# Eight of sixteen gates by Strassen's scheme in a third pass of the values' stage, and the first products of an output between the last head's jobs

## The chip, the cores and the metric

The kernel runs on one core of a Trainium2 chip. The metric is the device time of one launch in microseconds (us). The engines are named as in the profile: PE multiplies matrices, DVE (VectorE) and ACT (ScalarE) work on elements and empty PE's accumulators (PSUM), POOL and SP here mostly issue transfers.

## What is computed

One layer of a decoder on 1024 tokens of width 1024. The part that matters here, cut from the reference:

```python
h = rms_norm(x, pre_mix_g[l])
proj = h @ w_in[l]
qa, ka, va, qb, kb, vb, gates = jnp.split(proj, split_at, axis=-1)
oa = diff_attention(rope(qa), rope(ka), va, lam)        # A: 4 heads, two softmaxes each
ya = (rms_norm(oa, diff_head_g[l]) * (1.0 - lam_init)).reshape(b, s, A_WIDTH) @ w_a_out[l]
outs, lses = [], []                                     # B: 3 dilations x 4 heads
for g, (window, dil) in enumerate(B_PAIRS):
    o_g, lse_g = dilated_group(rope(qb)[:, :, g], rope(kb)[:, :, g], vb[:, :, g], window, dil)
...
yb = (softmax over g of lses, times outs).reshape(b, s, B_WIDTH) @ w_b_out[l]
g_a, g_b = jnp.split(jax.nn.sigmoid(gates), 2, axis=-1)
x = x + rms_norm((g_a * ya + g_b * yb) @ w_mix_out[l], post_mix_g[l])
... # then a conv-gated MLP, not touched by the change
```

The gates are 2048 columns of `proj`: `g_a` (the first output's) is 1024 of them, `g_b` the others.

## The kernel before

Every large product is made of three float32r matmuls (`mm3`, lines 155 to 157): each operand is held as a rounded high part and a low part, and high x high, low x high and high x low are summed in one PSUM bank. ACT makes the high part, DVE the low one (`split`, line 148; `L149` and `L146` in the profile). A full matmul is 128x128 weights against 512 columns.

The span falls into stages that follow each other.

The values' stage (0 to about 165 us of the span) makes the attention's values by Strassen's scheme: seven products `p1` to `p7` in place of eight, each of four steps k. A table `steps_v` sets the order. It runs two passes, i = 0 and i = 1, of 1024 columns each. `fetch_v` loads the weights' blocks, `ready_v` combines and splits them, `step_v` does the matmuls, and at k = 3 `take_v` empties the four banks into `quarter` tiles, which `put_v` scales and stores on POOL's queue to `v_d`.

Attention A (about 205 to 538 us) runs four heads, each of eight jobs `attend_a(h, i)`, i being a block of 128 queries. A job computes scores `s` on PE into one of two PSUM buffers (`L759`, `L760`, chunks of up to 512 keys), DVE masks them and takes the maximum while it copies them out (`L762`), ACT takes the exponential (`L771`), DVE combines the two softmaxes (`L778`), PE transposes the result (`L691`, `pt<-ident,s`), ACT and DVE split it, and PE multiplies it by the values (`L704`, `L707`). The norm of half a head (`head_norm`) has a sum over partitions on PE (`L833`, `o<-ones,sq`), a chain of small DVE operations (`L166` to `L179`), a spread (`L836`) and a product (`L842`).

Between the jobs stand pieces of independent products, the fills: the next head's projections (`proj_a`, letter p; each has 192 matmuls `acc<-xh` and `acc<-xl`), the first projection of attention B (P), and gates (g, 48 matmuls each, evacuated by DVE at `L250` and stored to `gt_d`). `A_FILLS` lists the fills of each head; `START_GATES` gates run ahead of the first head. `interleave` spreads the fills over the jobs by weight, and a scheduler orders each engine's instructions from priorities and its own estimate of times.

Attention B (about 538 to 870 us) has twelve steps of four jobs `attend_b`, with the next step's projection (`proj_b`) as fill, and `B_GATES` gates in the last one. Its results go through DRAM and are merged over the dilations (`merge`: load statistics `mr`, weights `me`, store them to `e_d`, load them back broadcast as `mw`, multiply and add in two halves; `L1054` to `L1089`), then split to `obh` and `obl`. The first output's products (`branch(a["w_a_out"], ...)`, `ya`, `L1190`) run after the last step's jobs; steps of the merge are called between them by numbers (`later(n, fn)`). Then come the second output, the mix and the MLP.

Three lines that set the order around the change:

```python
START_GATES, A_FILLS, B_GATES = 1, ("gpgg", "gpvgg", "wgpgg", "xgPVgg"), 3
steps_v += [(p, i, k) for i in range(2) for p in ("p1", "p5", "p6", "p7", "p4", "p3") if i or p != "p1" for k in range(4)]
for i, fn in zip((3, 5, 7, 11, 16), merge(BH - 1, ob)):
```

Of the kernel before, what the change touches and what calls it, by code (L numbers as in the profile page):

```python
# [54 lines left out]
XT_BUFS, NORM_AT, ANGLES_AT, SINES_AT, TABLES_AT, STORE_AT = 6, 14, 25, 33, 34, {35: 0, 37: 3, 39: 2, 41: 1}  # L55

# [6 lines left out]
def plan():  # L63

    order = []
    for h in range(AH):
        order += [QA + h * P, KA + h * P]
    for h in range(BH):
        for g in range(BG):
            order += [QB + g * 512 + h * P, KB + g * 512 + h * P]  # L70
    order += [GT + i * P for i in range(2 * KC)]
    return order
# [15 lines left out]
def trunk(ctx: ExitStack, tc: tile.TileContext, a, out):  # L88
# [355 lines left out]

    with ExitStack() as st_y:
# [3 lines left out]
        steps_v = [(p, 0, k) for k in range(4) for p in ("p2", "p1")] + [("p2", 1, k) for k in range(4)]  # L449
        steps_v += [(p, i, k) for i in range(2) for p in ("p1", "p5", "p6", "p7", "p4", "p3") if i or p != "p1" for k in range(4)]  # L450
        wz = [t[:, k % 2] for t in [wv.tile([P, 2, 512], F32, tag=f"wz{i}", name="wz") for i in range(2)] for k in range(2)]
# [37 lines left out]
        def take_v(p, i, m, ps):  # L489
# [3 lines left out]
            def copy(to, r):  # L493
                if i:
                    nc.scalar.activation(to, ps, AF.Copy, scale=r)
                else:
                    nc.scalar.activation(to, ps, AF.Copy)

            def add(to, r):
                if i:  # L500
                    plus(to, ps, r, to, ALU.add)
                else:
                    tt(to, ps, to, ALU.add)
# [5 lines left out]
            if p == "p6":  # L509
                copy(quarter[1, i][m], r1)  # L510
            if p == "p7":
                copy(quarter[3, i][m], r1)
            if p == "p4":
# [4 lines left out]
        def put_v(q, i, scale):  # L518

            c, j = q // 2, q % 2  # L520
            for m in range(4):
# [6 lines left out]
        banks, fifth = {}, {}  # L528

        def step_v(n):  # L530
# [16 lines left out]
            if p == "p7":  # L547
                for m in range(4):
                    r, y = rstd[:, 4 + m : 5 + m], quarter[3, i][m]
                    if i:  # L550
                        plus(y, banks[False][m], r, y, ALU.add)
                    else:
                        tt(y, banks[False][m], y, ALU.add)

# [50 lines left out]
        yw = open_pool(st_y, "yw")  # L605
        made, fetched, again = 12, 14, []
        quarter.update({(q, 0): new_y(f"b{q}", yw) for q in range(1, 4)})
        for n in range(8, len(steps_v)):
# [23 lines left out]
            if n == TABLES_AT:  # L632
                turn_norms()
            if (p, i, k) == ("p6", 1, 0):
                quarter[1, 1] = new_y("a0")
                quarter[3, 1] = new_y("b3", yw)
                quarter[2, 1] = new_y("b2", yw)
            step_v(n)
            if k == 3 and i and p in ("p1", "p7", "p4"):
                put_v({"p1": 0, "p7": 3, "p4": 2}[p], 1, p == "p1")  # L640
            if (p, i) == ("p5", 1):

                again.append(load_raw(a["xT"][k][:, 512:], next(tags)))
            if (p, i) == ("p6", 1):
                with behind_marks():
                    split_x(k, halves()[1], again[k])
        put_v(1, 1, False)
    st_v.close()
# [69 lines left out]
    def proj_a(h, res):  # L718
# [128 lines left out]

    free_gates = list(range(2 * KC))

# [34 lines left out]
    def once(fn):  # L884

        fn()
        yield 0
# [234 lines left out]
    for n, (pair, g, h) in enumerate(steps[:-1]):  # L1122
# [3 lines left out]
        if h % 2:  # L1126
            fetch_b(*nxt[:2])
        fill = proj_b(nxt[1], nxt[2], ops_b[nxt], functools.partial(split_b, *nxt[:2]) if h % 2 else None)
        interleave(jobs(todo), 4, (itertools.chain(fill, once(load_ots)) if nxt == steps[-1] else fill, 8))
        if pair == 1 and g < 2 and h == 2:  # L1130
# [5 lines left out]
    oa = [[slot(n) for _ in range(AH)] for n in ("oah", "oal")]  # L1136
    load_o(oa, None, 0, 1, ots[0])
    load_o(oa, None, 1, 1, ots[1])
    later(1, lambda: load_o(oa, oa_d, 2, 2, ots[0]))
    later(1, lambda: load_o(oa, oa_d, 3, 2, ots[1]))  # L1140
    ob = []
# [5 lines left out]
    xs.close()  # L1147


    st_o = ExitStack()  # L1150
    st2 = ExitStack()
    ym = open_pool(st2, "ym")
    ya = [ym.tile([P, S], F32, tag=f"y{d}", name=f"ya{d}") for d in range(KC)]
    mid_b = open_pool(st_o, "mid_b")
    ob += [[mid_b.tile([P, S], F32R, tag=f"{n}{h}", name=n) for h in range(BH)] for n in ("obh", "obl")]

    def branch(w_out, o, first, gate_tile, get_psum, scale=None):

        gts = []
        for d2 in range(KC // 2):  # L1160
            wh, wl = load_unit(w_out[d2], scale=scale)
            for e in range(2):
                d = 2 * d2 + e
                while len(gts) < min(d + 3, KC):
                    gts.append(gate_tile())
                    side(gts[-1], gt_d[first + len(gts) - 1])
                with behind_marks():
                    nc.scalar.activation(gts[d], gts[d], AF.Sigmoid)
            for half, sl in enumerate(halves()):
                for e in range(2):  # L1170
                    ps = get_psum()
                    for k in range(4):
                        w = slice(k * 256 + e * P, k * 256 + (e + 1) * P)
                        mm3(ps, wh[:, w], wl[:, w], o[0][k][:, sl], o[1][k][:, sl], k == 0, k == 3)
                    yield 2 * d2 + e, half, sl, ps, gts[2 * d2 + e]


    for h in range(2):
        load_o(ob, ob_d, h, 3 * h + 4)
    for i, fn in zip((3, 5, 7, 11, 16), merge(BH - 1, ob)):  # L1180
        later(i, fn, 0)

# [5 lines left out]

    for d, half, sl, ps, gt in branch(a["w_a_out"], oa, 0, gate_slot, psum, ghead):
        marks["DVE"] = nc.vector.tensor_tensor(ya[d][:, sl], ps, gt[:, sl], op=ALU.mult).ins  # L1190
        clock[0] += 1
        while due and due[0][0] <= clock[0]:
            do_due()
# [18 lines left out]
    with st2:  # L1212
        wm = open_pool(st2, "wm", side="right")
        us = [None] * 8
        with st_o:
# [4 lines left out]

            for d, half, sl, ps, gt in branch(a["w_b_out"], ob, KC, gate_tile, any_psum):
                nc.vector.tensor_tensor(gt[:, sl], ps, gt[:, sl], op=ALU.mult)
                nc.gpsimd.tensor_tensor(gt[:, sl], gt[:, sl], ya[d][:, sl], op=ALU.add)
                split(mh[:, d, sl], ml[:, d, sl], gt[:, sl])
                for i in MIX_UNITS.get(d, ()) if half else ():

                    to = (wm, ("mh", "ml"), 4) if i < 4 else (ym, (f"y{2 * i - 8}", f"y{2 * i - 7}"), 1)
                    us[i] = load_unit(a["w_mix_out"][i], *to)
# [467 lines left out]
def layout(inp):  # L1696
# [8 lines left out]
    w = f["w_in"][0]  # L1705
    arr["w_v"] = np.concatenate([w[:, VA:QB], w[:, VB:GT]], 1).reshape(KC, P, 2048)
    us = []
# [33 lines left out]
```

## Time and profile before

| what | us |
| --- | --- |
| median of 3 runs | 1707.98 (1705.85 to 1708.24) |
| the profiled execution, its own time | 1705.22 |
| its span, first to last instruction | 1703.2 |
| PE busy | 1683.8 (99%) |
| DVE busy | 1346.0 (79%) |
| ACT busy | 888.4 (52%) |
| POOL busy | 108.7 (6%) |

The span is shorter than the execution's time by 2.0 us. Matmuls overlap: a row of matmuls gives the time from the start of one to its end, and the rate is read from how many start in a window. Idle time of an engine costs something only where PE, busy for 99% of the span, then waits too.

### The profile page before, as it was taken

To read this page: it belongs to the slowest core of one execution; us is meant where nothing else is said; L and a number is where in the kernel's file an instruction comes from. 1 tells how busy PE (TensorE), PEld (TensorE's weight loads), DVE (VectorE), ACT (ScalarE), POOL (GpSimd) and SP (SyncE) were. 2 spreads that over 40 slices of the span, in tenths; PEclk is the share of its full clock that TensorE was granted. 3 is DMA by queue.
4 is the path that set the end of the run, shared out by engine and by line. 5 is a ranking of instruction groups with operands and counts; after the bars stand their busy time and mean duration, and the time that the engine had idled before them with its cause. 6 is when DMAs were issued, how large, how long until landed. Compare 5 with 4: busy or idle time off the path is not lost.

```text
span 1703.2 us, 23027 instructions
## 1 busy us (share of the span) xinstructions
PE 1683.8 (99%) x8076; PEld 1408.2 (83%) x8076; DVE 1346.0 (79%) x2557; ACT 888.4 (52%) x1631; POOL 108.7 (6%) x174
## 2 busy tenths in 40 slices
PE   9999999999999999999999999999999999999997
PEld 7887888888888888888878788888888888888886
DVE  8895686877777776678756865899999999799977
ACT  7634574655544776667553443454444434355453
POOL 0031000000000000000123400300000000000000
PEclk9999999999999999999999999999999999999999
DMA  8677321214112213243675631122222222296624
GB/s 270 228 231 253 98 63 62 83 59 119 50 63 81 69 57 108 81 123 107 214 259 193 198 112 75 38 99 91 95 80 81 81 93 93 79 345 214 202 76 160
DMA packets 104451, 216.41 MB, mean 127 GB/s; under 512 B 12992, under 2 KB 22144, under 8 KB 104336
## 3 DMA queue, kind: packets, MB, share of 16 engines
q1 hardware_dynamic: 89296, 171.28, 30.5%
q0 software_dynamic: 10288, 35.28, 6.2%
q10 hardware_dynamic: 4752, 8.39, 1.3%
q8 instruction: 63, 1.03, 0.2%
q14 instruction: 52, 0.43, 0.1%
HBM read 167.05 MB, written 47.86 MB: 126 GB/s over the span
## 4 chain that ended last, share of the span: by engine, by line
PE 89%; DMA 5%; DVE 3%; issue 2%; ACT 1%; POOL 1%; SPq 0%; DVEq 0%; ACTq 0%; POOLq 0%
PE acc L155 20%; PE acc L157 19%; PE acc L156 19%; PE acc L1577 3%; PE acc L1576 3%; PE acc L1575 3%; PE o L704 2%; PE pt L691 2%; PE acc L1256 2%; PE acc L1254 2%; PE acc L1255 2%; PE o L707 1%; PE s L156 1%; PE s L157 1%; PE s L155 1%
## 5 line engine op out<-in xcount | busy, mean ns | idle before, releaser
L155 PE MATMUL acc<-xh,whi 128*128 128x512 f32 x768 | 304.2, 396 | 0.0
L157 PE MATMUL acc<-xl,whi 128*128 128x512 f32 x768 | 303.8, 396 | 0.0
L156 PE MATMUL acc<-xh,wlo 128*128 128x512 f32 x768 | 303.1, 395 | 0.0
L149 ACT ACTIVATE whi<-raw 128x512 fp32r<-128x512 f32 (+1 forms) x252 | 155.9, 626 | 185.9 <-PE acc L157 107.6
L146 DVE TENSOR_TENSOR wlo<-raw,whi 128x512 fp32r<-128x512 f32 (+1 forms) x252 | 180.7, 723 | 44.2 <-ACT whi L149 40.5
L157 PEld LDWEIGHTS acc<-xl,whi 128*128 128x128 f32 x768 | 144.4, 188 | 27.7
L156 PEld LDWEIGHTS acc<-xh,wlo 128*128 128x128 f32 x768 | 144.5, 188 | 27.6
L155 PEld LDWEIGHTS acc<-xh,whi 128*128 128x128 f32 x768 | 144.4, 188 | 27.4 <-DVE t L679 0.2
L155 PE MATMUL acc<-mh,whi 128*128 128x512 f32 x400 | 155.8, 390 | 0.3 <-ACT mh L149 0.3
L156 PE MATMUL acc<-mh,wlo 128*128 128x512 f32 x400 | 155.6, 389 | 0.0
L157 PE MATMUL acc<-ml,whi 128*128 128x512 f32 x400 | 155.3, 389 | 0.0
L678 ACT ACTIVATE t<-acc 64x512 f32<-64x512 f32 (+1 forms) x160 | 94.7, 592 | 58.5 <-PE acc L157 56.6
L1452 DVE TENSOR_TENSOR u<-acc,u 128x512 f32<-128x512 f32 x133 | 90.4, 683 | 22.7 <-PE acc L157 22.6
L149 ACT ACTIVATE whi<-s 128x512 fp32r<-128x512 f32 x76 | 46.9, 627 | 102.1 <-PE acc L157 88.0
L679 DVE TENSOR_TENSOR t<-acc,cos 128x512 f32<-128x512 f32 x64 | 44.2, 690 | 58.8 <-ACT t L678 58.0
L155 PEld LDWEIGHTS acc<-mh,whi 128*128 128x128 f32 x400 | 75.1, 188 | 15.9 <-ACT mh L149 0.5
L157 PEld LDWEIGHTS acc<-ml,whi 128*128 128x128 f32 x400 | 75.1, 188 | 15.7
L156 PEld LDWEIGHTS acc<-mh,wlo 128*128 128x128 f32 x400 | 75.1, 188 | 15.6
L1576 PE MATMUL acc<-whi,wlo 128*128 128x512 f32 x220 | 77.6, 390 | 0.0
L1575 PE MATMUL acc<-whi 128*128 128x512 f32 x220 | 76.3, 389 | 0.0
L1577 PE MATMUL acc<-wlo,whi 128*128 128x512 f32 x220 | 73.2, 390 | 0.0
L762 DVE CUSTOM_DVE_ANT_0 s<-s,mask_a 128x512 f32<-128x512 f32 (+3 forms) x96 | 51.9, 553 | 23.3 <-PE s L760 14.6
(385 smaller groups left out, 3942.6 us busy)
## 6 DMA issues: line engine op xcount, KB each, us to landing
raw<-in_w_in SPq DMA_DIRECT2D x96, 256.0 KB, 2.9
raw<-in_w_up SPq DMA_DIRECT2D x88, 256.0 KB, 2.8
raw<-in_w_v SPq DMA_DIRECT2D x71, 256.0 KB, 4.7
raw<-c_d SPq DMA_DIRECT2D x48, 256.0 KB, 3.6
c_d<-c SPq DMA_DIRECT2D x22, 512.0 KB, 2.8
raw<-in_w_down SPq DMA_DIRECT2D x37, 256.0 KB, 4.5
v_d<-yv POOLq DMA_DIRECT2D x32, 256.0 KB, 5.5
gt_d<-gate ACTq DMA_DIRECT2D x32, 256.0 KB, 2.1
```

The source lines that it names most:

```text
L146: eng.tensor_tensor(lo, src, hi.bitcast(F32), op=ALU.subtract)
L149: copy = nc.scalar.activation(hi, src, AF.Copy)
L155: nc.tensor.matmul(o, sh, mh, start=first, stop=False, skip_group_check=on)
L156: nc.tensor.matmul(o, sl, mh, start=False, stop=False, skip_group_check=on)
L157: nc.tensor.matmul(o, sh, ml, start=False, stop=last, skip_group_check=on)
L678: nc.scalar.activation(t1[dst], ps[src], AF.Copy)
L679: nc.vector.tensor_tensor(t2, ps, cos[:, sl], op=ALU.mult)
L762: nc.vector.tensor_tensor_reduce(out=s_sb[:, c0:c1], in0=ps, in1=mask, scale=1.0, scalar=-3.0e38, op0=ALU.add, op1=ALU.max, accum_out=mx[: ...
L1452: nc.vector.tensor_tensor(to, made(p), x, op=ALU.add)
L1575: nc.tensor.matmul(banks[m], gh[:, tk], wh, start=f == 0, stop=False)
L1576: nc.tensor.matmul(banks[m], gl[:, tk], wh, start=False, stop=False)
L1577: nc.tensor.matmul(banks[m], gh[:, tk], wl, start=False, stop=f == NH - 1)
```

## The change

The values' stage gets a third pass, i = 2, which makes the eight gates of the first output by the same seven products. There the operands of `mm3` change places (the gates are wanted transposed), `put_g` multiplies the quarters by the row norm and stores them to `gt_d` on POOL's queue. The passes i = 1 and i = 2 run two products at a time in turns, so that the last step of one stands well ahead of the first step that reuses its banks. `w_v` is widened by these 1024 columns, and the same columns leave the layout of `w_in`. Loads of 256 KB from `w_v` go from 71 to 107, those from `w_in` from 96 to 80. Of the eight gates that are left, none runs ahead of the first head, seven are fills of attention A (there were 12 with the one ahead of it), and one runs in attention B's last step (there were 3).

In attention A the duplicated low halves of k (16 subtractions on DVE, 64x512) become copies on ACT. In attention B's last step four outputs (48 matmuls) of the first output's `branch` stand between the jobs, behind the gate; the rest of that generator runs after the jobs. Its sigmoids thus stand among the last exponentials, and ACT's table loads go from 9 to 11. The numbers of the last head's merge become 3, 5, 6, 9 and 12. In the second output the four banks of the first two columns are begun with k < 3 before the last head's product k = 3 (`late=True`).

```diff
-START_GATES, A_FILLS, B_GATES = 1, ("gpgg", "gpvgg", "wgpgg", "xgPVgg"), 3
+A_FILLS, B_GATES, B_OUTS = ("gpg", "gpvg", "wgpg", "xgPV"), 1, 4
...
+        for i in (1, 2):
+            steps_v += [("p1", 1, k) for k in range(4)] if i == 1 else turns(2, (0, 0, 1, 0, 1, 0, 1, 1), "p2", "p1")
+            steps_v += turns(i, (0, 0, 1, 0, 1, 0, 1, 1), "p5", "p6") + turns(i, (0, 0, 1, 1, 1, 1, 0, 0), "p3", "p7")
+            steps_v += [("p4", i, k) for k in range(4)]
...
+        def put_g(q):
+
+            c, j = q // 2, q % 2
+            for m in range(4):
+                y, sl = quarter[q, 2][m], halves()[j]
+                tt(y, y, rstd_row[:, sl], ALU.mult)
+                nc.gpsimd.dma_start(gt_d[c * 4 + m][:, sl], y)
...
-                mm3(use[m], x[0][:, k, tk], x[1][:, k, tk], wh, wl, k == 0 and p in ("p1", "p2", "p5"), k == 3, p in ("p6", "p7", "p4", "p3"))
+                ops = (x[0][:, k, tk], x[1][:, k, tk], wh, wl) if i < 2 else (wh[:, tk], wl[:, tk], x[0][:, k], x[1][:, k])
+                mm3(use[m], *ops, k == 0 and p in ("p1", "p2", "p5"), k == 3, p in ("p6", "p7", "p4", "p3"))
...
-            for part, kk, ll in ((u, k0, l0), (v, k1, l1)):
-                for to in (u, v):
-                    nc.vector.tensor_tensor(ll[to, sl], t[part], kk[part, sl].bitcast(F32), op=ALU.subtract)
+            for part, other, kk, ll in ((u, v, k0, l0), (v, u, k1, l1)):
+                nc.vector.tensor_tensor(ll[part, sl], t[part], kk[part, sl].bitcast(F32), op=ALU.subtract)
+                nc.scalar.activation(ll[other, sl], ll[part, sl].bitcast(F32), AF.Copy)
...
-        run(gates(START_GATES)[0])
...
+            if late and d2 == 0:
+                for half, e in todo:
+                    begun[half, e] = get_psum()
+                    products(d2, half, e, range(3), begun[half, e])
...
-    interleave(jobs(todo), 4, gates(B_GATES))
+    outputs, size = outputs_a(), 4 * B_GATES + B_OUTS
+    interleave(jobs(todo), 4, (part(outputs, size), size))
...
-    for i, fn in zip((3, 5, 7, 11, 16), merge(BH - 1, ob)):
+    for i, fn in zip((3, 5, 6, 9, 12), merge(BH - 1, ob)):
...
-            for d, half, sl, ps, gt in branch(a["w_b_out"], ob, KC, gate_tile, any_psum):
+            for d, half, sl, ps, gt in branch(a["w_b_out"], ob, KC, gate_tile, any_psum, late=True):
```

Where the order of instructions changes is seen at two places. The first is the border of heads 1 and 2 in attention A. On PE before, from the sum of a head's norm (`o<-ones,sq`) on, the matmuls `acc<-xh` and `acc<-xl` of the fills stand between the scores' chunks `s<-k,q`:

```order
L833 MATMUL o<-ones,sq 128x1 x4
L759 MATMUL s<-k_2977,q_2975 128x128
L760 MATMUL s<-l_2979,q_2975 128x128
L156 MATMUL acc<-xh,wlo 128x512
L157 MATMUL acc<-xl,whi 128x512
L155 MATMUL acc<-xh,whi 128x512
L156 MATMUL acc<-xh,wlo 128x512
L759 MATMUL s<-k_2978,q_2976 128x512
L760 MATMUL s<-l_2980,q_2976 128x512
L157 MATMUL acc<-xl,whi 128x512
L155 MATMUL acc<-xh,whi 128x512
L156 MATMUL acc<-xh,wlo 128x512
```

On PE after, the chunks of head 2's first jobs follow one another, with nothing between but one norm's transposes (`spread`), transposes of the last jobs of head 1 and their products with the values:

```order
L780 MATMUL s<-k_3463,q_3461 128x384
L781 MATMUL s<-l_3465,q_3461 128x384
L780 MATMUL s<-k_3462,q_3460 128x512
L781 MATMUL s<-l_3464,q_3460 128x512
L780 MATMUL s<-k_3462,q_3460 128x512
L781 MATMUL s<-l_3464,q_3460 128x512
L862 MATMUL pt<-ident,spread 128x128 x4
L712 MATMUL pt<-ident,s 128x128 x3
L780 MATMUL s<-k_3463,q_3461 128x512
L781 MATMUL s<-l_3465,q_3461 128x512
L725 MATMUL o<-pt,vh 128x256
L780 MATMUL s<-k_3463,q_3461 128x512
```

On DVE after, at the same place, the masks (`s,mx<-s,mask_a`) stand among the splits of the next values (`vl`), of transposes (`pt`) and of head 3's q, and the combination of 896 keys:

```order
L783 ISA s,mx<-s,mask_a 128x512
L783 ISA mx 128x1
L783 ISA s,mx<-s,mask_a 128x512
L783 ISA mx 128x1
L147 TENSOR_TENSOR vl<-vperm,vh 128x1024
L747 TENSOR_TENSOR q_4220<-t_4291,q_4220 64x512
L799 SCALAR_TENSOR_TENSOR s<-s,ratio 128x896
L748 TENSOR_TENSOR q_4221<-t_4291,q_4221 64x512
L747 TENSOR_TENSOR q_4220<-t_4393,q_4220 64x512
L787 TENSOR_TENSOR mx<-mx 128x2
L748 TENSOR_TENSOR q_4221<-t_4393,q_4221 64x512
L783 ISA s,mx<-s,mask_a 128x512
```

A chunk's matmuls can start only when the mask of the chunk two before it has emptied the buffer; what moved out from between them is independent work of PE.

The second place is the end of head 3, where attention B begins (`s<-kh,qh` are B's scores, which have no fill ahead of them either). On PE before, fills go on past the seventh of the eight sums of A's norms:

```order
L833 MATMUL o<-ones,sq 128x1 x4
L155 MATMUL s<-kh,qh 128x256
L156 MATMUL s<-kh,ql 128x256
L157 MATMUL s<-kl,qh 128x256
L157 MATMUL acc<-xl,whi 128x512
L155 MATMUL acc<-xh,whi 128x512
L156 MATMUL acc<-xh,wlo 128x512
```

On PE after, the next fill behind the same sum stands only after products with the values, the norm's transposes and those of the next block:

```order
L725 MATMUL o<-pt,vh 128x256 x2
L728 MATMUL o<-pt,vl 128x256
L725 MATMUL o<-pt,vh 128x256 x2
L725 MATMUL o<-pt,vh 128x128 x2
L728 MATMUL o<-pt,vl 128x128
L728 MATMUL o<-pt,vl 128x256
L862 MATMUL pt<-ident,spread 128x128 x4
L712 MATMUL pt<-ident,s 128x128 x3
L156 MATMUL acc<-xh,whi 128x512
```

The gates that were this head's last fills are gone from it, and its projection stands further ahead.

More of the change, by code (lines that the diff above doesn't have):

```diff
@@ L70, in plan @@
             order += [QB + g * 512 + h * P, KB + g * 512 + h * P]
-    order += [GT + i * P for i in range(2 * KC)]
+    order += [GT + i * P for i in range(KC, 2 * KC)]
     return order
@@ L510, in take_v @@
                 copy(quarter[1, i][m], r1)
+            if p == "p5" and i:
+                copy(quarter[3, i][m], r1)
             if p == "p7":
-                copy(quarter[3, i][m], r1)
+                (add if i else copy)(quarter[3, i][m], r1)
             if p == "p4":
@@ L546, in step_v @@
                     take_v(p, i, m, use[m])
-            if p == "p7":
+            if p == "p7" and i == 0:
                 for m in range(4):
[L549 to L553, printed above, removed]
+                    tt(quarter[3, 0][m], banks[False][m], quarter[3, 0][m], ALU.add)
         with ExitStack() as st0:
@@ L1127, in trunk @@
             fetch_b(*nxt[:2])
-        fill = proj_b(nxt[1], nxt[2], ops_b[nxt], functools.partial(split_b, *nxt[:2]) if h % 2 else None)
-        interleave(jobs(todo), 4, (itertools.chain(fill, once(load_ots)) if nxt == steps[-1] else fill, 8))
+        between = load_ots if nxt == steps[-1] else functools.partial(split_b, *nxt[:2]) if h % 2 else None
+        interleave(jobs(todo), 4, (proj_b(nxt[1], nxt[2], ops_b[nxt], between), 8))
         if pair == 1 and g < 2 and h == 2:
@@ new lines, in trunk, with gate_slot, outputs_a @@
+    first_gls = iter(("cos", "sin"))
+    def gate_slot():
+        tag = next(first_gls, None)
+        return tabs.tile([P, S], F32, tag=tag, name="gl") if tag else slot("gl", dt=F32)
+    def outputs_a():
+        yield from gates(B_GATES)[0]
+        xs.close()
+        ym.append(open_pool(st2, "ym"))
+        ya.extend(ym[0].tile([P, S], F32, tag=f"y{d}", name=f"ya{d}") for d in range(KC))
+        mid_b = open_pool(st_o, "mid_b")
+        ob.extend([mid_b.tile([P, S], F32R, tag=f"{n}{h}", name=n) for h in range(BH)] for n in ("obh", "obl"))
+        for d, half, sl, ps, gt in branch(a["w_a_out"], oa, 0, gate_slot, psum, ghead):
+            marks["DVE"] = nc.vector.tensor_tensor(ya[d][:, sl], ps, gt[:, sl], op=ALU.mult).ins
+            yield 1
@@ L1142, in trunk, with part @@
+    def part(gen, size):
+        while size > 0:
+            n = next(gen)
+            size -= n
+            yield n
+    for i in range(2):
+        load_o(oa, None, i, 0, ots[i])
+        do_due()
+    for i in range(2):
+        load_o(oa, oa_d, 2 + i, 1, ots[i])
     for i, fn in zip((1, 2, 3, 5, 9), merge(2, ob)):
@@ L1145, in trunk @@
     todo = [functools.partial(attend_b, g, h, jj, ops_b[pair, g, h], vs_b[pair, g], sbs) for jj in range(4)]
-    interleave(jobs(todo), 4, gates(B_GATES))
[L1147 to L1175, printed above, removed]
+    outputs, size = outputs_a(), 4 * B_GATES + B_OUTS
+    interleave(jobs(todo), 4, (part(outputs, size), size))
     for h in range(2):
-        load_o(ob, ob_d, h, 3 * h + 4)
-    for i, fn in zip((3, 5, 7, 11, 16), merge(BH - 1, ob)):
+        load_o(ob, ob_d, h, 3 * h + 3)
+    for i, fn in zip((3, 5, 6, 9, 12), merge(BH - 1, ob)):
         later(i, fn, 0)
-    first_gls = iter(("cos", "sin"))
-    def gate_slot():
-        tag = next(first_gls, None)
-        return tabs.tile([P, S], F32, tag=tag, name="gl") if tag else slot("gl", dt=F32)
-    for d, half, sl, ps, gt in branch(a["w_a_out"], oa, 0, gate_slot, psum, ghead):
-        marks["DVE"] = nc.vector.tensor_tensor(ya[d][:, sl], ps, gt[:, sl], op=ALU.mult).ins
+    for _ in outputs:
         clock[0] += 1
```

75 lines of the change are left out of this document (53 added, 22 removed).

## The prediction

> **What bounds the kernel.** I read the page first: busy shares, the throttle's clock, the chain that ended last.
>
> ```profile
> span 1703.2 us, 23027 instructions
> PE 1683.8 (99%) x8076; PEld 1408.2 (83%) x8076; DVE 1346.0 (79%) x2557; ACT 888.4 (52%) x1631; POOL 108.7 (6%) x174
> PEclk9999999999999999999999999999999999999999
> PE 89%; DMA 5%; DVE 3%; issue 2%; ACT 1%; POOL 1%; SPq 0%; DVEq 0%; ACTq 0%; POOLq 0%
> ```
>
> PE is busy for 99% of the span at an undisturbed clock, and the chain lies on it. So every matmul removed shows in full, and every new wait of PE costs in full. The second view is the waits of PE, the three longest groups:
>
> ```profile
> PE acc L155 <- ACT xh L371: 2.3, 2, 1.4
> PE acc L155 <- DVE ya L1190: 2.2, 3, 0.9
> PE acc L155 <- ACT yv L495: 1.9, 2, 1.3
> ```
>
> The first is the span's beginning, the second stands in the first output, the third in the values' stage. There is none in attention. The third view is busy time by windows (PE, PE's loads, DVE, ACT, POOL, clock, DMA): attention A as a whole, the border of heads 1 and 2, a stretch of the MLP with full matmuls only; then the border again with PE's matmuls into `acc` alone.
>
> ```profile
> 204.70:537.50 332.80, 332.80 (x1739) 283.81 (x1737) 256.06 (x692) 184.35 (x357) 1.14 (x4) 1.00 0.23 74
> 384.00:410.00 26.00, 26.00 (x145) 22.39 (x144) 23.44 (x65) 17.37 (x31) 0.00 (x0) 1.00 0.51 142
> 1300.00:1400.00 100.00, 100.00 (x443) 82.81 (x442) 92.08 (x122) 42.37 (x58) 1.10 (x11) 1.00 0.25 82
> 384.00:410.00 26.00, 20.14 (x81) 14.28 (x80) 2.06 (x4) 2.36 (x4) 1.00 0.51 142
> ```
>
> The third row gives the rate: 100 / 443 = 0.226 us for a matmul of 512 columns. The second and fourth carry my argument: at the border DVE is busy for 23.44 of 26 us although 81 fill matmuls (18.3 us of PE) stand there. Attention's own work keeps DVE, not PE, busy; the fills are PE's share of that time.
>
> **What is saved.** Strassen's third pass has 7 products x 4 steps x 4 tiles x 3 = 336 matmuls, the eight gates had 8 x 48 = 384: 48 x 0.226 = 10.8 us less, all on PE. The turns let banks be emptied under the other product, which removes the 1.9 us behind `yv`; the bounds are 0 and 1.9, I take 1.9. Sum -12.7. The third pass itself brings 36 loads and 16 stores of 256 KB: its work on DVE and ACT is like that of the second pass, where PE stayed busy but for that wait, so nothing is added; the stores on POOL's queue follow the values' and are read only at the outputs.
>
> **What the fills covered.** Attention A loses five gates, 240 matmuls or 54.2 us of PE. DVE loses ten evacuations and 16 subtractions, about 0.6 us each, 15.6 us. PE would be busy for 278.6 us, DVE for 240.5: 86% instead of 77%. That is below PE on the mean, so what decides is the places where no fill is left. I priced DVE's instructions there by its rows in attention A; instructions overlap, which a run of three shows.
>
> ```profile
> L762 DVE CUSTOM_DVE_ANT_0 s<-s,mask_a 128x512 f32<-128x512 f32 x48 | 32.9, 687 | 18.9 <-PE s L760 11.1 <-PE pt L691 7.3
> L762 DVE CUSTOM_DVE_ANT_0 s<-s,mask_a 128x384 f32<-128x384 f32 x16 | 8.7, 551 | 1.4 <-PE s L760 1.0
> L762 DVE CUSTOM_DVE_ANT_0 s<-s,mask_a 128x256 f32<-128x256 f32 x14 | 5.8, 419 | 0.2 <-PE pt L691 0.2
> L762 DVE CUSTOM_DVE_ANT_0 s<-s,mask_a 128x128 f32<-128x128 f32 x15 | 4.3, 285 | 1.8 <-PE s L760 1.8
> L146 DVE TENSOR_TENSOR pt<-pt 128x512 fp32r<-128x512 f32 x23 | 15.4, 685 | 2.5 <-ACT pt L149 2.5
> L146 DVE TENSOR_TENSOR pt<-pt 128x384 fp32r<-128x384 f32 x14 | 7.7, 551 | 0.1
> L146 DVE TENSOR_TENSOR vl<-vperm,vh 128x1024 fp32r<-128x1024 f32 x4 | 4.9, 1217 | 0.0
> L778 DVE SCALAR_TENSOR_TENSOR s<-s,ratio 128x896 f32<-128x896 f32 x4 | 4.6, 1150 | 0.1
> L778 DVE SCALAR_TENSOR_TENSOR s<-s,ratio 128x512 f32<-128x512 f32 x3 | 2.3, 753 | 0.1
> L778 DVE SCALAR_TENSOR_TENSOR s<-s,ratio 128x384 f32<-128x384 f32 x4 | 2.5, 618 | 0.1
> L778 DVE SCALAR_TENSOR_TENSOR s<-s,ratio 128x256 f32<-128x256 f32 x3 | 1.4, 478 | 0.0
> L778 DVE SCALAR_TENSOR_TENSOR s<-s,ratio 128x128 f32<-128x128 f32 x3 | 1.0, 349 | 0.1
> L727 DVE TENSOR_TENSOR q<-t,q 64x512 fp32r<-64x512 f32 x6 | 4.1, 686 | 0.2
> L836 DVE COPY spread<-rhy 128x512 f32<-128x512 f32 x6 | 2.5, 424 | 0.1
> L872 DVE TENSOR_TENSOR ql<-t,qh 128x512 fp32r<-128x512 f32 x2 | 1.4, 688 | 0.7 <-ACT qh L871 0.7
> L177 DVE SCALAR_TENSOR_TENSOR rhy<-rhw,rhy 128x4 f32<-128x4 f32 x18 | 2.9, 160 | 0.3
> ```
>
> ```profile
> 898.54 1.28 DVE L1190 TENSOR_TENSOR ya<-acc,gl 128x512 f32<-128x512 f32 x2
> 506.06 0.71 PE L691 MATMUL pt<-ident,s 128*128 128x128 f32 x5
> ```
>
> Two evacuations of about 0.68 us take 1.28: each instruction gives back 0.08 to the next. Five transposes take 0.71 with the last one's latency; I count 0.11 each.
>
> Place (a), the border of heads 1 and 2. A score's chunk needs one of two buffers, so it waits for the mask of the chunk two before. From the mask of head 2's third chunk to the mask that frees the buffer of its eleventh, DVE after has 6 masks of 512 (4.12) and one of 384 (0.55), two `vl` (2.43), the combination of 896 (1.15), a split of 384 (0.55), four `q` (2.74), the spread (0.42), the norm's product (taken as 0.69) and 12 small ones (1.92): 14.6 less 29 x 0.08, 12.3 us. PE's own work between the same two chunks has no fill: five chunks of 512 in two matmuls each (2.26), one of 384 and one of 128 (0.45), nine transposes (1.0), products with values (0.5), sums and starts (0.5), 4.7 us. PE must wait 7.6. On top come steps that wait for each other (mask, exponential, combination); the upper end is the 23.44 us of DVE less 7.7 (26 less 18.3) of PE's own work, 15.7. I take 8.5, near the count.
>
> Place (b), the end of head 3. The fill's next bank is freed by DVE's rotation of a projection of B, the last of 51 instructions from head 3's mask of 384 on: masks (two each of 512, 384, 256, 128) 3.88, splits (three of 512, two of 384) 3.16, combinations (512, 384, 256, 128) 2.20, two `vl` 2.43, two `ql` 1.38, spread and rotation (taken as 0.69) 1.11, 28 small ones 4.48, less 51 x 0.08: 14.6. PE has 10.2 us of its own in that stretch: A's chunks 2.3, B's 1.2, products with values 3.1, 24 transposes 2.6, four fill matmuls 0.9, a sum 0.1. The wait is at least 4.4. With few jobs left to alternate, DVE itself waits for exponentials, so I set the upper end at twice the count, 9, and take 6.5.
>
> Place (c), B's first steps, where some 60 instructions of PE after have no fill:
>
> ```profile
> 575.00:600.00 25.00, 24.98 (x158) 22.08 (x158) 22.75 (x52) 20.07 (x45) 0.00 (x0) 1.00 0.30 100
> ```
>
> DVE's slack there is 2.25 us of 25. If 20 of its fills (4.5 us) are missing, PE waits 2.3; bounds 0 (the projections of B still stand there) and 5 (twice that); I take 2.5. The same count made for the rows of before gives no wait, as its trace has none. Sum +17.5, with 12.0 as the sum of the counts.
>
> **The last merge.** Before, the last product with values, the weights' first and last steps, the load of `mw` and the first finished half stood so:
>
> ```profile
> 868.92 0.28 PE L707 MATMUL o<-pt,vl 128*128 128x128 f32 x1
> 890.57 0.16 DVE L1054 TENSOR_TENSOR mm<-mr 128x8 f32<-128x8 f32 x1
> 898.31 0.32 DVE L1066 TENSOR_TENSOR me<-me,mm 128x8 f32<-128x8 f32 x3
> 907.37 1.76 DVE L1086 TENSOR_TENSOR mw<-og,mw 128x1536 f32<-128x1536 f32 x1 [5.77 <-DMA mw<-e_d]
> 912.83 0.69 DVE L146 TENSOR_TENSOR obl<-om,obh 128x512 fp32r<-128x512 f32 x1
> ```
>
> ```profile
> v_d<-yv POOLq DMA_DIRECT2D x32, 256.0 KB, 5.5
> ```
>
> It took 44.6 us to the end of that half's split (913.5). After, 87 matmuls of the first output and 36 of the second that need no last head follow the last values: 123 x 0.226 = 27.8 us of cover, where 189 matmuls (42.7 us) stood by the order before. The chain's steps are called earlier. Statistics in two transfers like POOL's 5.5 us (11 for 21.7) and weights in 4 for 7.7 leave 30.2 of the 44.6, an estimate. That is 2.4 us late, about what is won if the 2.2 us for `ya` go, since the products between the jobs give ACT time for the sigmoids; together 0, between -2.2 (no lateness) and +5 (a third of the shortening fails). Two more table loads on ACT lie in its idle time there.
>
> **Sum.** -12.7 + 17.5 + 0 = +4.8. The profiled execution took 1705.22 us (span and 2.0 around it), 2.8 below the median of the runs; 1707.98 + 4.8 is 1713 us, own range 1709 to 1717.
>
> **Rivals.**
> Counts only: the scheduler's order leaves no more than 7.6, 4.4 and 0. For it speaks that attention before ran with DVE at 90% at a border and no wait; against it, that a count leaves out every step in which the engines wait for each other. -12.7 + 12.0 = -0.7: 1707.
> Faster: only (a) bites, since at (b) PE arrives later than I count, and the output's 2.2 go. -12.7 + 7.6 - 2.2 = -7.3: 1700.7. It decides if the waits in attention stay under 9.3 us. Against it: the rows of (b) are in a fixed order too.
> A late merge: the chain keeps 5 us more than its cover. +9.8: 1718. For it: cover falls by 15 us.
> A slowed clock: PE's waits are now several us long, and the clock falls behind them.
>
> ```profile
> 0.00:3.00 3.00, 1.75 (x4) 1.49 (x5) 0.37 (x2) 1.49 (x2) 0.70 (x6) 1.00 0.29 72
> 6.00:9.00 3.00, 2.17 (x10) 1.45 (x8) 0.80 (x2) 1.34 (x3) 0.00 (x0) 1.00 0.92 323
> ```
>
> With PE idle for 0.83 of 3 us the granted clock was 1.00; a wait of several us is not in the trace. If three such stretches of 3 us ran at half speed, each would lose 1.5, so +4.5 on the forecast: 1717. The Trainium skill, "TensorE: Matmul & The Clock Gate", section "Part 1: The HAM clock gate (the "warmup" mystery)", states this rule: an idle window of about 3.4 us halves the clock until about 3.4 us were busy. By its figure, three losses would be 5.1 us, an estimate. The trace disagrees so far as it goes: the very first 3 us, with PE idle for 1.25 of them, show 1.00 too.
>
> **Chances.** Forecast 0.33, counts only 0.26, faster rival 0.20, late merge 0.14, clock 0.07. The measurement tells 0.2%, 3.4 us: same is 1704.6 to 1711.4. Nearly all of the faster rival and a tenth of the counts are faster, 0.22; nine tenths of the counts and a quarter of the forecast are same, 0.32; the rest, 0.46, is slower. The range 1701 to 1720 holds all cases but the outer half of the faster one and the worst merges.
>
> **What would show it.** Of the changed kernel's trace: PE's waits in attention A of about 15 us, on masks (`s`) near the border of heads 1 and 2 and on the rotation at the end of head 3, beside 0 before; a values' stage without waits on `yv`; DVE near 86% in attention A; the second output's beginning with a wait on `obl` or none. The prediction is wrong if those waits sum to under 9 us, or if the granted clock falls.

## The result: slower by 1.4%

The changed kernel took 1731.28 us (median, 1727.88 to 1732.26) against 1706.91 for the kernel before; the ratio is 1.014 with a 95% interval of 1.0122 to 1.0158. The prediction said 1713, range 1701 to 1720. Its direction held and its size did not. The page of the profiled execution after (1727.88 us):

```profile
span 1726.1 us, 23087 instructions
PE 1690.7 (98%) x8028; PEld 1412.6 (82%) x8028; DVE 1360.3 (79%) x2581; ACT 917.2 (53%) x1677; POOL 118.5 (7%) x190
PE   9999999999898999999999999999999999999997
PEclk9999999999899999999999899999999999999999
PE 89%; DVE 5%; DMA 2%; ACT 2%; issue 1%; POOL 0%; SPq 0%; DVEq 0%; ACTq 0%; POOLq 0%
```

PE has 48 matmuls fewer (8076 to 8028) and is yet busy for 6.9 us more. The row of the throttle shows why: its eleventh slice and its twenty-third are below 9. The chain now has 5% on DVE instead of 3%.

PE's waits, of the whole span (line waited at, releaser: us in total, times, longest):

```profile
PE s L780 <- DVE mx L783: 4.0, 4, 2.3
PE acc L156 <- DVE gl L1274: 3.8, 1, 3.8
PE pt L862 <- DVE spread L857: 3.7, 2, 3.1
PE pt L712 <- ACT bs L997: 3.0, 3, 1.4
PE acc L156 <- ACT obh L150: 2.3, 1, 2.3
PE acc L156 <- ACT yv L509: 0.3, 1, 0.3
```

The first and third stand in attention A, the fourth in attention B, the second and fifth at the beginning of the second output. The wait behind `yv` has shrunk from 1.9 to 0.3, and those in the first output (`ya`, 2.2) are gone. By windows (PE, PE's loads, DVE, ACT, POOL, granted clock, DMA):

```profile
425.00:450.00 25.00, 19.56 (x83) 15.32 (x82) 22.52 (x74) 14.53 (x27) 0.00 (x0) 0.73 0.20 54
550.00:575.00 25.00, 21.71 (x101) 18.87 (x102) 19.99 (x53) 14.51 (x29) 2.03 (x4) 0.80 0.22 71
600.00:625.00 25.00, 22.36 (x138) 19.86 (x136) 18.58 (x49) 19.07 (x49) 0.00 (x0) 0.86 0.20 65
945.00:960.00 15.00, 9.47 (x27) 7.11 (x28) 13.09 (x17) 12.23 (x19) 6.46 (x5) 0.66 0.41 139
```

These are the places (a), (b) and (c) of the prediction and the second output's beginning, (d). In each PE waits, and in each the granted clock is below 1. Two more windows cut place (a):

```profile
428.00:436.00 8.00, 5.33 (x28) 3.31 (x26) 6.92 (x29) 5.33 (x9) 0.00 (x0) 1.00 0.09 35
436.00:450.00 14.00, 11.23 (x35) 9.22 (x36) 13.63 (x36) 8.11 (x14) 0.00 (x0) 0.51 0.23 59
```

For 8 us PE is busy for two thirds of the time at full clock; then the clock stands at half for 14 us, in which DVE is busy for 13.63 of 14. The longest wait at each of the places (a) to (c), with the releaser in brackets, and for (a) also the longest one before its clock fell:

```profile
434.05 0.50 PE L780 MATMUL s<-k,q 128*128 128x512 f32 x1 [1.06 <-DVE mx L783]
443.78 0.80 PE L780 MATMUL s<-k,q 128*128 128x512 f32 x1 [2.30 <-DVE mx L783]
559.73 1.09 PE L862 MATMUL pt<-ident,spread 128*128 128x128 f32 x4 [3.09 <-DVE spread L857]
612.93 0.33 PE L712 MATMUL pt<-ident,bs 128*128 128x128 f32 x1 [1.44 <-ACT bs L997]
```

I summed, over windows of 2 us, PE's busy time x (1 - clock) as the time lost by the clock:

| place | waits of PE, us | lost by the clock, us |
| --- | --- | --- |
| (a) heads 1 and 2, 425 to 450 | 5.3 | 5.4 |
| (b) end of head 3, 546 to 566 | 4.6 | 4.6 |
| (c) B's first steps, 606 to 622 | 2.5 | 3.2 |
| (d) last jobs and second output, 890 to 960 | 7.5 | 3.2 |

PE's idle time rose by 14.4 us over the kernel before (24.9 against 10.5 in the first 1100 us), the clock took 16.4, and 48 matmuls x 0.226 gave back 10.8: +20.0 of the 22.9 by which the spans differ. (The waits of the table sum to 19.9, more than the rise of 14.4, because waits of before, on `yv`, `ya` and a few shorter ones, are gone.) Another 1.4 lie behind the last matmul; 1.5 I don't place.

### The profile page after: what moved, and what is told of

It reads as the page before. It is cut to its first block, busy times and chain, and to the rows that moved or that the text cites. A ratio compares the mean times of both kernels' runs of the same rounds, so it can differ in the third digit from the quotient of the medians.

```text
span 1726.1 us, 23087 instructions
## 1 busy us (share of the span) xinstructions
PE 1690.7 (98%) x8028; PEld 1412.6 (82%) x8028; DVE 1360.3 (79%) x2581; ACT 917.2 (53%) x1677; POOL 118.5 (7%) x190
## 4 chain that ended last, share of the span: by engine, by line
PE 89%; DVE 5%; DMA 2%; ACT 2%; issue 1%; POOL 0%; SPq 0%; DVEq 0%; ACTq 0%; POOLq 0%
PE acc L156 19%; PE acc L157 19%; PE acc L158 19%; PE acc L1629 3%; PE acc L1628 3%; PE acc L1627 3%; PE o L725 2%; PE pt L712 2%; PE acc L1307 2%; PE acc L1308 2%; PE acc L1306 2%; PE s L158 1%; PE s L157 1%; PE s L156 1%; PE o L728 1%
## 5 line engine op out<-in xcount | busy, mean ns | idle before, releaser
L156 PE MATMUL acc<-xh,whi 128*128 128x512 f32 x652 | 260.3, 399 | 0.3 <-ACT yv L509 0.3
L157 PE MATMUL acc<-xh,wlo 128*128 128x512 f32 x652 | 259.0, 397 | 0.0
L158 PE MATMUL acc<-xl,whi 128*128 128x512 f32 x652 | 258.9, 397 | 0.0
L156 PEld LDWEIGHTS acc<-xh,whi 128*128 128x128 f32 x652 | 124.0, 190 | 24.3 <-ACT yv L509 0.8
L158 PEld LDWEIGHTS acc<-xl,whi 128*128 128x128 f32 x652 | 123.7, 190 | 24.1
L157 PEld LDWEIGHTS acc<-xh,wlo 128*128 128x128 f32 x652 | 123.9, 190 | 23.7
L725 PE MATMUL o<-pt,vh 128*128 128x256 f32 (+1 forms) x376 | 67.5, 278 | 2.1 <-DVE pt L147 1.2
```

The lines of the kernel that those rows point to most:

```text
L156: nc.tensor.matmul(o, sh, mh, start=first, stop=False, skip_group_check=on)
L157: nc.tensor.matmul(o, sl, mh, start=False, stop=False, skip_group_check=on)
L158: nc.tensor.matmul(o, sh, ml, start=False, stop=last, skip_group_check=on)
L725: nc.tensor.matmul(o[:, q0 : q1 + 1], vs[b // 4][0][:, b % 4, c], t[:, part], start=first and n == part == 0, stop=False)
```

## The experiments

The theory was: attention A's and B's DVE and ACT work used to be hidden by fills, and where none stands PE waits and its clock halves. The rivals were the third pass itself (loads, stores), the new order of the outputs, and waits that follow from the order rather than from DVE's amount of work.

**Five gates ahead, nothing else.** The kernel before, in which twelve gates are fills of attention A and one more runs ahead of its first head, with

```diff
-START_GATES, A_FILLS, B_GATES = 1, ("gpgg", "gpvgg", "wgpgg", "xgPVgg"), 3
+START_GATES, A_FILLS, B_GATES = 6, ("gpg", "gpvg", "wgpg", "xgPV"), 3
```

> The kernel before with nothing changed but the place of five gates: six gates instead of one run ahead of the first head, seven instead of twelve are fills of attention A. As many matmuls as before, no third pass, the output as before. If the changed kernel loses its time because attention A is left without fills (waits of 12.4 us there in its trace, and a granted clock of 0.73, 0.80 and 0.86 in three windows of 25 us, another 15 us or less): 1722 to 1734 us, with the same waits on masks and the norm's spread and a halved clock behind them. If the third pass, its loads or its stores cost the time, or the output's new order: 1707 us.

Measured: 1743.22 us against 1708.67, ratio 1.0203 (1.0187 to 1.022). With the same matmuls as before and no third pass it lost more than the change did. Its windows at places (a), (b) and (c):

```profile
425.00:450.00 25.00, 21.77 (x81) 16.57 (x79) 23.93 (x60) 14.55 (x26) 0.00 (x0) 0.73 0.25 74
540.00:565.00 25.00, 19.35 (x106) 16.91 (x107) 22.29 (x69) 15.81 (x35) 1.98 (x4) 0.80 0.16 53
600.00:625.00 25.00, 22.50 (x137) 19.84 (x135) 20.83 (x53) 19.89 (x50) 0.00 (x0) 0.86 0.11 36
```

The clock falls at the same three places. (The windows are laid over the place in each kernel, so that the means agree to two digits is partly chance; the clock took 6.1, 3.9 and 3.1 us there, and 5.4, 4.6 and 3.2 in the changed kernel.) So the missing fills suffice, and the third pass is not needed for the loss. The time lies 9 us above the range I gave. The trace shows two things that I had not counted, waits of 4.8 us on `ya` (2.2 before) and 3.0 us lost by the clock in the mix; that DVE still has the 16 subtractions may add to it.

**The third pass at half width, all other gates as fills of attention A.** From the changed kernel, with the rest of the edit left out here:

```diff
-A_FILLS, B_GATES, B_OUTS = ("gpg", "gpvg", "wgpg", "xgPV"), 1, 4
+A_FILLS, B_GATES, B_OUTS = ("gpg", "gpvgg", "wgpgg", "xgPVggg"), 0, 0
...
+            at, wd = (2 * i * 512, 512) if i < 2 else (2048, 256)
...
-    free_gates = list(range(KC, 2 * KC))
+    free_gates = list(range(KC // 2, 2 * KC))
```

> The changed kernel with the third pass over 512 columns (four gates, 24 matmuls saved) and the other twelve gates all as fills of attention A, so that no stretch of PE without a fill is longer than 3 us in its order; the output's part as before. If missing fills are the cause: no waits in attention, clock 1.00 there, and 24 x 0.226 + 1.9 = 7.3 us saved, 1697 to 1702 us. If the third pass itself costs time: above 1707 us.

Measured: 1714.22 us, ratio 1.0034 (1.0022 to 1.0045). By its number this is the second case, a third pass that costs time, but the trace does not show its reason: up to 26 us PE waits as it does before, and from there to 860 us its only wait is one of 1.0 us, on `sq` in attention A. The mechanism in attention was right, the time was not, and the loss was elsewhere:

```profile
425.00:450.00 25.00, 25.00 (x143) 21.74 (x142) 18.09 (x49) 9.74 (x21) 0.00 (x0) 1.00 0.25 86
540.00:565.00 25.00, 25.00 (x122) 20.92 (x121) 16.24 (x35) 11.70 (x19) 1.14 (x4) 1.00 0.30 95
860.00:875.00 15.00, 12.50 (x58) 10.15 (x58) 9.78 (x42) 9.71 (x25) 3.71 (x6) 0.77 0.82 302
930.00:945.00 15.00, 9.77 (x27) 7.22 (x28) 13.09 (x17) 11.82 (x19) 6.20 (x5) 0.66 0.47 171
```

In attention A no clock is lost again. But no gate is left for the last head's jobs, and PE now waits there and at the second output, with 6.7 us lost by the clock. Before, gates stood in both regions; here all twelve went to the first.

**The outputs' old order.** The changed kernel with `B_OUTS` 0, the merge's numbers 3, 5, 7, 11, 16, and without `late=True`.

> The changed kernel with the output's part of before: no first outputs between the last jobs, the merge's old numbers, the second output not begun early. If the waits of 6.1 us at the second output's beginning and the halved clock behind them come from the new order there: 1718 to 1723 us, without those waits. If they come from the merge's chain being late whatever the order: 1728 to 1735 us, waits on the same tiles. The places in attention A stay as they are in both.

Measured: 1727.64 us, ratio 1.011 (1.0093 to 1.0128), between the two ranges. PE waits 5.0 us on `obh` and 1.7 on `gl`, where the changed kernel waited 2.3 and 3.8. So the new order is not what makes place (d). What differs is the gates left for the last head's jobs: with three (before, and the kernel with five gates ahead) there is no wait on `obh`; with one (5.0 and 2.3) or none (2.6, at half width) there is. That is a comparison of kernels that differ in other things too; the number of gates alone was not varied, so this cause of (d) is not shown. Whether the new order costs a little is open as well: the intervals of the two ratios (1.0093 to 1.0128 here, 1.0122 to 1.0158 for the changed kernel) just overlap.

**Lighter and heavier DVE.** Three kernels change DVE's work and leave PE's matmuls as they are. The values' low halves on POOL (`split(*res[-1], v, nc.gpsimd)`):

> The changed kernel with the low halves of the values (four of 128x1024 in attention A, 1.22 us each on DVE) made on POOL instead. If DVE's sum of work sets the waits at the borders of heads 1 and 2 and at the end of head 3: 2 to 2.4 us less of wait at each, and less time at half clock, 1720 to 1728 us. If DVE's order and the steps that wait for each other set it: 1729 to 1733 us. If POOL is slow (1.55 us for 512 columns of its one like instruction) and the values come late: above 1733 us.

Measured: 1734.97 us, ratio 1.0155 (1.0138 to 1.0171), in the range given for a slow POOL. POOL took 2.48 us for each, twice DVE's 1.22, and the order changed with it; the waits moved (place (a) 3.2 instead of 5.3, place (b) 8.8 instead of 4.6). It tells little of the cause. So I left the subtraction out and let POOL write zeros:

```diff
-                split(*res[-1], v)
+                nc.scalar.activation(res[-1][0], v, AF.Copy)
+                nc.gpsimd.memset(res[-1][1].bitcast(F32), 0.0)
```

> The changed kernel with the low halves of the values left out: POOL writes zeros in place of DVE's subtraction (1.22 us each; two at each of the first two places), PE multiplies as before. If DVE's sum of work at a place sets PE's wait there: some 2.4 us less wait at the borders of heads 1 and 2 and at the end of head 3, less time at half clock, 1719 to 1727 us. If the wait is set by steps that wait for each other, or by the order alone: 1729 to 1733 us.

Measured: 1726.02 us, ratio 1.0114 (1.0098 to 1.0129), in the range given for the sum of DVE's work, but only in part for its reason. At place (a) the waits fell from 5.3 to 3.6 us and the loss by the clock from 5.4 to 3.0; at (b) the waits rose, 4.6 to 5.3; at (c), where two of these subtractions stand too, the waits rose from 2.5 to 3.1 and the loss by the clock fell from 3.2 to 1.6. So the gain came at (a) and (c), and more of it through the clock than through the waits. The other way, the duplicated low halves of k back on DVE:

> The changed kernel with the duplicated low halves of k back on DVE (16 subtractions of 0.68 us more on DVE, 16 copies fewer on ACT). If DVE sets the waits: a few of them fall into the uncovered places, 1733 to 1741 us, with waits in attention above 12.4 us. If not: 1729 to 1733 us.

Measured: 1734.49 us, ratio 1.016 (1.0147 to 1.0174), and 16.2 us of waits in attention, as expected if DVE sets them. Against the changed kernel the interval of each of these two kernels overlaps, so neither shows much alone. Against each other, 1726.02 (1725.81 to 1728.11) and 1734.49 (1734.07 to 1735.37), both measured against the same runs of before, they are 8.5 us apart. That speaks for the amount of DVE's work, though the scheduler's order changed with it; and the amount does not set the wait at each place, since at (b) less work did not shorten it.

**One gate made twice**, as a further fill of head 1 (`"gpvgg"`):

> The changed kernel with one gate of the second output made twice, as a further fill of head 1 in attention A (48 matmuls, 10.8 us of PE, and two evacuations more); the place at the border of heads 1 and 2 is covered again by the order, the two later ones are not. If PE loses there what the trace shows (5.3 us of waits and 6.5 us at half clock), the added work is nearly free: 1726 to 1733 us, and no fall of the clock near 440 us. If that place costs only its waits or nothing: 1736 to 1742 us.

Measured: 1739.65 us, ratio 1.0178 (1.0162 to 1.0194): the added 10.8 us were not free, they cost 8.4 (6.3 if each is taken against its own runs of before, 1708.94 and 1706.91). This lies in the second of my ranges, but not for its reason, a place (a) that costs little: there waits and clock took 5.9 us instead of 10.7 (the expectation's 6.5 us at half clock are 5.4 lost by the sum over windows). At (b), where the order shifted, they took 13.8 instead of 9.2, and that ate the gain. A fill added at one place shifts the scheduler's order at the next; the price of a place alone is not to be had this way.

**The clock by itself.** A kernel of nothing but bursts on PE that wait for DVE's reads, run once:

> A kernel that computes nothing of the layer: stretches of 100 full matmuls (22.6 us), and between them eight phases of bursts on PE, each waiting for DVE to have read the bank: bursts of 8, 16, 32, 4, 32, 32, 32 and 2 matmuls against 1, 1, 1, 1, 2, 4, 6 and 1 reads of 0.7 us. If the clock halves where PE's busy share over a few us is low, however short each wait: 0.5 in the phases of 8, 4 and 2 matmuls with one read (66%, 50% and 30% busy by 0.226 us a matmul and 0.9 us a wait) and 1.00 in those of 16 and 32 with one. If it takes one idle stretch of about 3.4 us, as the Trainium skill's rule has it ("TensorE: Matmul & The Clock Gate", "Part 1: The HAM clock gate (the "warmup" mystery)"): 1.00 in all phases but those with four reads (an estimate of 3 us of wait) or six (4.4 us).

One row for each of the phases of 8, 16 and 32 matmuls with one read, then most of the phase of 4, then that of 32 with two reads:

```profile
28.00:76.00 48.00, 34.74 (x133) 23.33 (x132) 11.68 (x17) 0.00 (x0) 1.00 0.00 0
99.00:148.00 49.00, 40.88 (x167) 30.70 (x168) 7.13 (x11) 0.00 (x0) 1.00 0.00 1
168.00:224.00 56.00, 50.54 (x215) 39.61 (x214) 4.81 (x7) 0.00 (x0) 1.00 0.00 1
252.00:308.00 56.00, 40.83 (x79) 23.25 (x80) 13.36 (x20) 0.00 (x0) 0.50 0.00 0
332.00:380.00 48.00, 40.66 (x173) 31.71 (x171) 6.70 (x10) 0.00 (x0) 1.00 0.00 0
```

Bursts of 8 with waits of 0.8 us (72% busy) leave the clock at 1.00, bursts of 4 with the same waits do not. The first four of those, in order of time (start, length, and the wait ahead in brackets):

```profile
243.76 1.20 PE L102 MATMUL s<-w 128*128 128x512 f32 x4 [0.78 <-DVE t L107]
...
247.72 1.19 PE L102 MATMUL s<-w 128*128 128x512 f32 x4 [0.78 <-DVE t L112]
249.69 1.86 PE L102 MATMUL s<-w 128*128 128x512 f32 x4 [0.78 <-DVE t L112]
```

After three bursts, some 6 us, the clock halves within the fourth (1.86 us; the later ones take 2.07), and it stays so to the phase's end. In the phase of 2 it halves at the third burst. So the first theory was right for 4 and 2 and wrong for 8; the second was wrong for 4 and 2, and right for the long waits: with four reads the clock fell too. Of that phase, the first burst and the second, each of 32 matmuls, with the wait ahead of it in brackets:

```profile
413.74 7.55 PE L102 MATMUL s<-w 128*128 128x512 f32 x32 [0.78 <-DVE t L107]
424.23 9.07 PE L102 MATMUL s<-w 128*128 128x512 f32 x32 [2.95 <-DVE t L112]
```

A wait of 2.95 us makes the burst behind it 1.5 us longer; a wait of 1.5 us (two reads) does not. So a wait of three us costs four and a half. With six reads, a wait of 4.39 us, a burst takes 9.13 to 9.17 us: the longer wait adds no more behind it.

One thing limits what the column of the granted clock can tell. It shows 1.00 from the first row on, while the first matmuls do not run at that rate. In this kernel the stretch that begins at 3.81 us has some 11 matmuls in 4 us, and later 20 in the same time:

```profile
4.00:8.00 4.00, 4.00 (x11) 3.14 (x12) 0.00 (x0) 0.00 (x0) 1.00 0.00 0
24.00:28.00 4.00, 4.00 (x20) 3.30 (x19) 0.00 (x0) 0.00 (x0) 1.00 0.00 0
```

In the first row the matmuls start 0.43 us apart up to about 7.3 us, as they do at half clock, and then 0.23.

**The turns alone.** The kernel before with its second pass in turns (and the changed `branch`, which loads the first output's gates in another order, without `late`), once with ACT's copies of k's low halves and once without. Two places of the edit, written as made from the changed kernel:

```diff
-A_FILLS, B_GATES, B_OUTS = ("gpg", "gpvg", "wgpg", "xgPV"), 1, 4
+A_FILLS, B_GATES, B_OUTS = ("gpgg", "gpvgg", "wgpgg", "xgPVgg"), 3, 0
...
-        for i in (1, 2):
+        for i in (1,):
```

> The kernel before with the products of its second pass in turns and the duplicated low halves of k copied by ACT, no third pass, its fills and its output as they were. If the turns remove the wait behind yv and nothing else moves: 1.9 us less, 1705 to 1707 us. If the other order of fills opens a stretch without them at attention B's first steps (5 us of PE in its order): 1709 to 1714 us, with waits and a lower clock near 580 us.

> The kernel before with the second pass in turns alone, the duplicated low halves of k left on DVE. If the turns made the gain seen with both (5.8 us, 2.5 to 7 by its interval): 1702 to 1706 us. If ACT's copies were a part of it: 1705 to 1709 us, with waits of PE on DVE in attention.

Measured: 1703.15 us against 1708.94, ratio 0.997 (0.9959 to 0.9981), with ACT's copies; 1700.55 against 1707.52, ratio 0.9961 (0.9949 to 0.9974), without. Both are faster than the kernel before and than the changed one, and both lie below all the ranges given; between the two the intervals overlap, so ACT's copies gained nothing that can be seen. The page and the two longest waits of the second one:

```profile
span 1698.1 us, 23030 instructions
PEclk9999999999999999999999999999999999999999
PE acc L156 <- ACT xh L372: 3.2, 2, 1.8
PE pt L591 <- DVE t4l L588: 1.2, 1, 1.2
```

The waits on `yv` (1.9) and on `ya` (2.2) are gone, the fills stand as before, and the clock does not fall. These waits are 4.1 of the 5.8 and 7.0 us gained; the rest I don't place. This is the part of the change that pays: the turns together with the other order of loads in `branch`, which were not tested apart.

## Why the prediction was right and wrong

**What is saved** held. 48 matmuls are gone, and the turns took 1.6 of the 1.9 us behind `yv`; the two kernels with the turns have no wait there. The third pass brought no new wait in the values' stage. The rate of 0.226 us was right at full clock.

**What the fills covered** was right in its places and near in size. Waits came at (a), (b) and (c), and nowhere else in attention but for 1.4 us at the last jobs: 5.3, 4.6 and 2.5 us, 12.4 in all, where I took 8.5, 6.5 and 2.5 and my counts of work alone gave 12.0. At (a) 3.8 of the 5.3 us end on the masks, as I had said, with DVE busy for 22.52 of 25 us. At (b) the longest one ends not on the rotation of a projection of B but on the spread of A's norm (3.09 us), a step of DVE too. At (c) the 2.5 us are luck: I had taken them from DVE's slack, but every wait there ends on ACT (`osb` and `bs`, the longest 1.44 us), and DVE was busy for only 18.58 of 25 us. The share that I forecast for DVE in attention A, 86%, did not come either: it was 76% (234.39 of 307.70 us, from the first score at 268.0 to the last norm's sum at 575.7), since I had divided DVE's work by PE's work alone and left out the time in which PE waits or runs slowly. At (a) the count (7.6) is above the measured wait. One reason can be seen: part of DVE's surplus was spent while PE ran its matmuls at half speed, so it shows as a slow PE and not as a wait. Waits and clock together are 10.7 there.

**The clock** is the step that failed. I gave a slowed clock 0.07 and nothing in the sum; it took 16.4 us, more than the rise of PE's idle time (14.4). I had argued from a row with PE idle for 0.83 of 3 us that the clock would stay, while my own sum forecast waits of several us, which that row could not speak for. The other row that I brought against the rival, the first 3 us at 1.00, says nothing at all: the column misses the start of a program, as the kernel of bursts shows, and in the kernel before the first full matmul (at 4.88 us) takes 0.77 us where later ones take 0.39. The Trainium skill, "TensorE: Matmul & The Clock Gate", section "Part 1: The HAM clock gate (the "warmup" mystery)", had the direction: idle time halves the clock until PE has been busy for a few us. The trace now agrees with that. It differs in the measure: 2.95 us of wait were enough, below the 3.4 us that the Trainium skill gives there, and so were waits of 0.8 us with short bursts between. Had I put that mechanism on my own 17.5 us of waits as I priced it, 1.5 us for each of three stalls, the result would have been 1717; it took about 4 us for each of four places, since the clock stayed down longer than I had priced: at (a) for 14 us, through a further wait of 2.30, and at (b) it fell twice, before and behind the wait of 3.09.

**The last merge** failed as a term too: I took 0 with an upper bound of 5, and the second output's beginning had waits of 6.1 us against the 2.2 on `ya` that went, with 3.2 us more by the clock. The first half's chain did shorten: 26.6 us from the last product with values (909.4) to its end (936.0), where I had estimated 30.2. What I had not followed is the work behind it:

```profile
942.78 1.76 DVE L1106 TENSOR_TENSOR mw<-og,mw 128x1536 f32<-128x1536 f32 x1 [6.73 <-DMA mw<-e_d]
946.02 0.63 ACT L150 ACTIVATE obh<-om 128x512 fp32r<-128x512 f32 x1 [10.70 <-DVE om L1109]
946.56 2.70 ACT L150 ACTIVATE whi<-raw 128x512 fp32r<-128x512 f32 x5
949.27 1.28 ACT L1183 ACT_TABLE_LOAD   x1
950.57 1.06 ACT L1183 ACTIVATE gl<-gl 128x1024 f32<-128x1024 f32 x1
952.40 0.80 PE L156 MATMUL acc<-obh,whi 128*128 128x512 f32 x1 [3.82 <-DVE gl L1274]
```

The second half is loaded only after the first is added. ACT stands idle for 10.70 us in front of its split, and behind that split in ACT's queue are five weight splits, the table load and the sigmoid of the gate without which DVE can't empty the first bank. PE waits 2.3 us for the half and 3.8 for the bank, and the clock falls. I had called the table loads covered by ACT's idle time; the idle time was there, but ahead of the split and not behind it.

**Range and chances.** Slower had the largest chance, 0.46. The range ended at 1720 because the rivals stood side by side: the late output and the slowed clock each had 1717 or 1718. They are not alternatives. A late output is itself a wait behind which the clock falls, so both came together with the forecast, and their sum was outside. That the waits in attention were 5 us less than I took hid a part of the miss.

## What to carry to other kernels

Independent products that fill the gaps of a dependent chain are not worth their matmuls alone: find the stretches where the other engines have more work than PE without them, place by place, before moving them. In these traces a wait of PE of about 3 us, or several us in which PE was busy for two thirds of the time or less, was mostly paid again at half clock: waits and clock together were 1.4 to 2.3 times the waits at the four places. When one cause feeds two rivals, give them a common case with the sum of both.

## What the runs showed of the hardware

The granted clock fell to 0.50 without any long wait: bursts of 4 matmuls with waits of 0.8 us (1.20 of each 1.98 us busy before it fell, 61%, by the trace's ends of matmuls) brought it down and held it there for 56 us, bursts of 8 (72%) never did, and at place (a), with no wait longer than 1.06 us before the fall, 67% over 8 us was followed by 14 us at half. This makes no sharp threshold: in the kernel with five gates ahead a single wait of 2.81 us in the first output, with PE busy for 53% of 6 us around it, left the clock at 1.00.

```profile
924.00:930.00 6.00, 3.19 (x15) 2.35 (x14) 4.40 (x10) 1.05 (x2) 0.75 (x1) 1.00 0.31 78
```

POOL's subtraction of 128x1024 took 2.48 us against 1.22 on DVE.
